# Where the lower part of a split weight is computed during the delta stage of a two-layer trunk: POOL instead of DVE

## The chip, the cores and the metric

The kernel runs on one core of a Trainium2 chip. The time is the device time of one execution in microseconds. Five engines work side by side, each through its own queue in order: PE (matrix products; its weight loads are shown apart as PEld), DVE (VectorE), ACT (ScalarE), POOL (GpSimd) and SP (which here only issues DMAs). They meet in SBUF and, for the products, in PSUM.

## The reference

Two layers over 512 latent and 256 context tokens of width 1024. Layer 0 mixes by a gated delta rule (16 value heads on 8 query/key heads of 128), layer 1 by retention; behind each stands a squared-ReLU network of width 4096. Everything is float32. What the change touches is layer 0's mixer:

```python
def gdn_mixer(hc, hl, w_in, conv_w, a_log, dt_bias, norm_g, w_out, need_ctx):
    proj = jnp.concatenate([hc, hl], axis=1) @ w_in
    qkv = proj[..., :GDN_CONV_DIM]
    z = proj[..., GDN_CONV_DIM:GDN_CONV_DIM + GDN_VALUE_DIM]
    ...
    qkv = jnp.concatenate([jax.nn.silu(short_conv(qkv[:, :n_ctx], conv_w)),
                           jax.nn.silu(short_conv(qkv[:, n_ctx:], conv_w))], axis=1)
    ...
    o = bidirectional_prefix_scan(q, k, v, g, beta, n_ctx).transpose(0, 2, 1, 3)
    ...
    y = (rmsnorm(o, norm_g) * jax.nn.silu(z)).reshape(o.shape[0], o.shape[1], GDN_VALUE_DIM) @ w_out
```

The scan works chunk by chunk. Inside a chunk it solves a unit lower triangular system, which the kernel does by inverting the triangle.

## The kernel before

**Split products.** PE multiplies in fp32r, which keeps fewer bits than float32. So every operand is split: `hi` is the value rounded to fp32r, `lo` the rest, and a product is the sum of three (hi·hi, hi·lo, lo·hi). `split` (L53) makes the two: ACT copies into `hi` (L56), DVE subtracts into `lo` (L57). For weights `w_cols` (L63) does that: it loads a block of 1024 rows and 128 columns in two halves (`raw`, 128 partitions by 512 elements, two buffers, loads on SP's queue at L72), and splits each half into a tile `hl` (three buffers). Attention to the names: `hl<-raw,hl` at L57 is the subtraction.

**The delta stage.** One call, `layer0_mix`, holds it. Its parts:

- `conv_tile` (32 times: 16 for keys and queries, 16 for values): `w_cols`, then 24 products of 512 columns into the PSUM tile `gl` and 24 of 256 into `gc`, both with two buffers (L91), then the short convolution: ACT scales one tap (L579), DVE adds three more, read straight from PSUM (L582).
- `z_tile` (16 times): the same products for the output gate, with one ACT function behind.
- `gdn_s2`, once for each pair of heads: products of keys and queries (L670), decay masks on DVE (L673, L679, L682), and the inversion of 32 by 32 triangles: their entries go through DRAM into the tile `u` (L695, L705), POOL clears the other half (L709, L711), and 30 steps of two DVE instructions each (L717, L720) follow, every one waiting for the one ahead. `gdn_iv` puts the small inverses together by products (from L754 on).
- `gdn_step`: 12 steps for each pair of heads (6 chunks in 2 directions) that carry the state. In them DVE makes `r` (L851) and `s` (L882), ACT `qs` and `und`, and POOL adds `qs` to the output of the other direction (L860).
- `gdn_y`, `gdn_y2`: norm of the output; its reciprocal root is taken on POOL (L114, tile `ms`), its product on DVE (L915), and PE transposes it (L921).

The code lists this work pair by pair with priorities (the scan first, then what the next pair needs, then projections to fill). A scheduler of the framework lays out each engine's order from the priorities and its own estimate of durations when the kernel is built, so a change of one instruction's engine changes the order on all engines. When the chip runs, each engine goes through its list strictly in order and waits wherever an operand isn't there.

Of the kernel before, what the change touches and what calls it, by code (L numbers as in the profile page):

```python
# [10 lines left out]
F32 = mybir.dt.float32  # L11
# [3 lines left out]
ALU = mybir.AluOpType  # L15
# [27 lines left out]
class Trunk:  # L43
# [6 lines left out]
            kw.setdefault("reuse_waits", "tile")  # L50
        return es.enter_context(self.tc.tile_pool(name=name, bufs=bufs, **kw))

    def split(self, hi, lo, src, scale=None):  # L53
        nc = self.nc
        if scale is None:
            nc.scalar.activation(out=hi, in_=src, func=AF.Copy)  # L56
            nc.vector.tensor_tensor(out=lo, in0=src, in1=hi.bitcast(F32), op=ALU.subtract)  # L57
        else:
            nc.scalar.activation(out=hi, in_=src, func=AF.Copy, scale=scale)
            nc.vector.scalar_tensor_tensor(  # L60
                out=lo, in0=src, scalar=scale, in1=hi.bitcast(F32), op0=ALU.mult, op1=ALU.subtract
            )

    def w_cols(self, src, parts=2):
        n = 8 // parts
        res = []
        for h in range(parts):
            raw = self.wraw.tile([128, n, 128], F32, tag="raw", name="raw")
            if callable(src):
                src(raw, h * n, n)  # L70
            else:
                self.nc.sync.dma_start(  # L72
                    out=raw, in_=src[h * n * 128:(h + 1) * n * 128].rearrange("(k p) f -> p k f", p=128))
            hl = self.whl.tile([128, 2, n, 128], F32R, tag="hl", name="hl")
            self.split(hl[:, 0], hl[:, 1], raw)
            res.append(hl)
        return lambda a, k: res[k // n][:, a, k % n, :]

# [209 lines left out]

    def layer0_mix(self):
        nc = self.nc  # L290
        es_a = ExitStack()
        es_b = ExitStack()
        self.psg = self.pool(es_a, "psg", space=PSUM)
# [5 lines left out]
        with ExitStack() as es:  # L299
# [4 lines left out]
            raw = mpool.tile([128, 8, T], F32, name="xraw")  # L304
# [35 lines left out]

        st = [{} for _ in range(8)]
        self.mark = {}
        free = ("kk0", "kk1", "uo0", "uo1")
        s1 = [self.gdn_s1(p, st[p], psk, scan, prep) for p in range(8)]
        sv = [self.gdn_sv(p, st[p], prep) for p in range(8)]
        s2 = [self.gdn_s2(p, st[p], psk, scan, prep, free if p == 0 else ("pp",) if p == 1 else ("kk0", "kk1", "uo0")) for p in range(8)]
        hi = lambda: self.tc.high_priority(PRI)
# [78 lines left out]
            fill_z()  # L426
        es_l.close()
        self.es_gdn = es_a

    def gemm_pair(self, w):  # L430
        pl = self.psg.tile([128, 512], F32, tag="gl", name="gl", bufs=2)
        self.gemm_t(pl, w, self.xt, NC_T, NL_T)
        pc = self.psg.tile([128, 256], F32, tag=self.gc[0], name="gc", bufs=self.gc[1])
        self.gemm_t(pc, w, self.xt, 0, NC_T)
        return ((pl, NC_T, NL_T), (pc, 0, NC_T))
# [942 lines left out]
```

## Time and profile before

| | |
|---|---|
| median of 3 runs | 2560.19 us (2559.29 to 2561.56) |
| profiled execution | 2564.44 us, span from the first to the last instruction 2562.7 us |
| mean granted PE clock | 0.980 |
| busy in the span: PE, DVE, ACT, POOL | 95%, 65%, 42%, 6% |
| delta stage with its projections | about 85 to 970 us of the span |

A line that names a source line, an engine and an operation stands for a group of instructions; `x` is their count, then come the busy time in us, the mean of one in ns, and behind the second bar the time that the engine idled just before them and whom it waited for. A line of windows gives a stretch (from:to and length in us) and the busy time of each engine in it with its number of instructions. Numbers such as `128x512` are partitions by elements of each.

### The profile page before, as it was taken

The numbers are of one execution on the slowest core, as the hardware profiler recorded it, in microseconds if no ns is written. First come the engines' busy times: TensorE is split into PE (matmuls) and PEld (weight loads), VectorE is DVE, ScalarE is ACT, GpSimd is POOL, SyncE is SP. The second block draws the span as 40 slices with busy tenths as digits, with TensorE's granted clock in tenths as the row PEclk, the third lists the DMA queues.
The fourth block names the chain that finished last, engine by engine and source line by source line (L and its number), as shares of the span: only waits on it lengthen the run. The fifth ranks groups of instructions, "written<-read, shape, count | busy, mean of one in ns | idle before, by whom it ended". The sixth has DMA issues, their size and how long they took to land.

```text
span 2562.7 us, 38997 instructions
## 1 busy us (share of the span) xinstructions
PE 2431.7 (95%) x14879; PEld 2010.7 (78%) x14879; DVE 1661.7 (65%) x3382; ACT 1074.0 (42%) x2357; POOL 163.7 (6%) x248
## 2 busy tenths in 40 slices
PE   8799798998888999999999999999999999999998
PEld 4687686786777787878888888888888887788887
DVE  5568767777776845887876667874353546644446
ACT  5576556565654553253222222653231322532222
POOL 1101111111201110000000000000000000000000
PEclk9899899899999999999999999999999999999999
DMA  6332324333132238354444444243122223433332
GB/s 211 89 96 77 106 51 113 80 105 94 43 109 67 74 113 272 132 165 132 132 144 129 123 130 129 100 135 93 50 84 61 78 66 115 150 97 91 107 91 91
DMA packets 346828, 276.94 MB, mean 108 GB/s; under 512 B 105608, under 2 KB 293488, under 8 KB 346640
## 3 DMA queue, kind: packets, MB, share of 16 engines
q1 hardware_dynamic: 345616, 271.30, 35.2%
q10 hardware_dynamic: 1024, 3.15, 0.5%
q8 instruction: 117, 1.92, 0.3%
q14 instruction: 71, 0.58, 0.1%
HBM read 241.72 MB, written 32.67 MB: 107 GB/s over the span
## 4 chain that ended last, share of the span: by engine, by line
PE 58%; DVE 5%; DMA 2%; ACT 2%; issue 1%; POOL 0%; SPq 0%; POOLq 0%; DVEq 0%; ACTq 0%
PE pn L940 22%; PE gl L91 14%; PE rvp L1257 5%; PE gc L91 3%; PE rl L91 3%; PE rgp L1257 3%; PE pv L1287 3%; PE sc L1265 1%; PE rc L91 1%; PE nps L276 1%; DVE hl L57 0%; DVE ma L199 0%; DMA zt<-zd 0%; PE mps L214 0%; PE uo L865 0%
## 5 line engine op out<-in xcount | busy, mean ns | idle before, releaser
L91 PE MATMUL gl<-xt,hl 128*128 128x512 f32 (+2 forms) x2760 | 704.6, 404 | 53.9 <-DVE acc L582 31.9
L91 PEld LDWEIGHTS gl<-xt,hl 128*128 128x128 f32 x2760 | 517.0, 194 | 161.9 <-issue 27.9
L57 DVE TENSOR_TENSOR hl<-raw,hl 128x1024 fp32r<-128x1024 f32 (+1 forms) x306 | 321.4, 1052 | 231.1 <-ACT hl L56 230.3
L56 ACT ACTIVATE hl<-raw 128x1024 fp32r<-128x1024 f32 (+1 forms) x306 | 280.0, 920 | 409.6 <-PE pn L940 251.9
L940 PE MATMUL pn<-hl,fh 128*128 128x512 f32 x1920 | 444.7, 391 | 2.2 <-DVE fh L1074 1.9
L940 PEld LDWEIGHTS pn<-hl,fh 128*128 128x128 f32 x1920 | 357.3, 188 | 80.0 <-DVE fh L1074 5.0
L91 PE MATMUL gc<-xt,hl 128*128 128x256 f32 x1944 | 273.2, 289 | 8.9 <-DVE acc L582 4.7
L91 PEld LDWEIGHTS gc<-xt,hl 128*128 128x128 f32 x1944 | 253.3, 193 | 19.9 <-ACT zs L442 5.5
L199 DVE SCALAR_TENSOR_TENSOR ma<-mraw,cst,ma 128x256 f32<-128x256 f32 x280 | 123.5, 482 | 40.4 <-DMA mraw<-in_w_mod 38.1
L940 PE MATMUL pn<-hl,yh 128*128 128x512 f32 x576 | 133.8, 392 | 2.5 <-ACT yh L56 1.4
L954 DVE TENSOR_TENSOR facc<-pn,facc 128x512 f32<-128x512 f32 x120 | 82.5, 689 | 81.8 <-PE pn L940 81.5
L1257 PE MATMUL rvp<-hl,xt 128*128 128x512 f32 x576 | 132.8, 389 | 0.0
L940 PEld LDWEIGHTS pn<-hl,yh 128*128 128x128 f32 x576 | 107.2, 188 | 26.8 <-ACT yh L56 2.6
L1257 PEld LDWEIGHTS rvp<-hl,xt 128*128 128x128 f32 x576 | 107.8, 188 | 22.2
L1071 ACT ACTIVATE fr<-gl 128x512 f32<-128x512 f32 x64 | 38.2, 597 | 193.3 <-PE gl L91 190.7
L582 DVE SCALAR_TENSOR_TENSOR acc<-gl,cw,acc 128x511 f32<-128x511 f32 (+1 forms) x96 | 71.6, 746 | 37.9 <-ACT acc L579 37.1
L940 PE MATMUL pn<-hl,ryt 128*128 128x512 f32 x384 | 92.0, 397 | 0.0
L1257 PE MATMUL rgp<-hl,xt 128*128 128x512 f32 x384 | 91.0, 393 | 0.0
L91 PE MATMUL rl<-xt,hl 128*128 128x512 f32 x384 | 89.5, 391 | 0.4 <-DVE hl L57 0.4
L717 DVE TENSOR_TENSOR tmp<-u 112x30 f32<-112x30 f32 (+14 forms) x240 | 81.5, 339 | 9.4 <-POOL u L709 6.2
L940 PEld LDWEIGHTS pn<-hl,ryt 128*128 128x128 f32 x384 | 71.6, 188 | 16.8
L91 PEld LDWEIGHTS rl<-xt,hl 128*128 128x128 f32 x384 | 71.5, 188 | 15.7 <-DVE hl L57 0.9
(282 smaller groups left out, 3347.9 us busy)
## 6 DMA issues: line engine op xcount, KB each, us to landing
raw<-in_w_ff SPq DMA_DIRECT2D x128, 512.0 KB
mraw<-in_w_mod SPq DMA_DIRECT2D x112, 256.0 KB
raw<-in_gdn_w_in SPq DMA_DIRECT2D x96, 256.0 KB
raw<-in_ret_w_in SPq DMA_DIRECT2D x32, 512.0 KB
mraw<-in_w_mod SPq DMA_DIRECT2D x24, 512.0 KB
e<-gd SPq DMA_DIRECT2D x32, 384.0 KB
mraw<-in_w_mod SPq DMA_DIRECT2D x8, 1024.0 KB
raw<-in_gdn_w_out SPq DMA_DIRECT2D x16, 512.0 KB
```

The source lines that it names most:

```text
L56: nc.scalar.activation(out=hi, in_=src, func=AF.Copy)
L57: nc.vector.tensor_tensor(out=lo, in0=src, in1=hi.bitcast(F32), op=ALU.subtract)
L91: nc.tensor.matmul(ps, lhsT=w(a, k), rhs=xt[:, b, k, t0:t0 + n], start=(k == 0 and i == 0), stop=(k == 7 and i == 2))
L199: eng.scalar_tensor_tensor(out=accs[v], in0=raw[:, k], scalar=c, in1=accs[v], op0=ALU.mult, op1=ALU.add)
L276: nc.tensor.transpose(ps[:, k, :], xn[:, (half * 4 + k) * 128:(half * 4 + k + 1) * 128], self.ident)
L582: nc.vector.scalar_tensor_tensor(out=acc[:, t0 + a:t0 + a + m], in0=ps[:, b:b + m], scalar=c[j], in1=acc[:, t0 + a:t0 + a + m], op0=ALU.mu ...
L717: nc.vector.tensor_tensor(out=t3, in0=u3[:, 0:c, c:c + 1].to_broadcast([112, c, n]), in1=u3[:, c:c + 1, c + 1:32].to_broadcast([112, c, n] ...
L940: m = nc.tensor.matmul(ps, lhsT=lhs(a, k, t), rhs=hls[hf][k // 2][:, b, k % 2], start=(k == 0 and n == 0), stop=(k == 3 and n == 2))
L954: nc.vector.tensor_tensor(out=dst, in0=ps, in1=dst, op=ALU.add)
L1071: nc.scalar.activation(out=r, in_=ps, func=AF.Relu)
L1257: nc.tensor.matmul(ps, lhsT=xt[:, a, kk, t * 128:(t + 1) * 128], rhs=hls[kk // 2][:, b, kk % 2], start=(kk == 0 and n == 0), stop=(kk == 7 ...
L1287: nc.tensor.matmul(pvs[it], lhsT=pts[jt][:, i, it * 128:(it + 1) * 128], rhs=v[:, j, jt], start=(jt == 0 and n == 0), stop=(jt == 5 and n ...
```

## The change

`split` takes an engine for the subtraction, and `w_cols` passes the one that stands in `self.lo_eng`. That is POOL from the first projection of the delta stage to its end, and DVE before and after it. The splits of activations and of other weights stay where they are.

```diff
-    def split(self, hi, lo, src, scale=None):
+    def split(self, hi, lo, src, scale=None, eng=None):
         nc = self.nc
         if scale is None:
             nc.scalar.activation(out=hi, in_=src, func=AF.Copy)
-            nc.vector.tensor_tensor(out=lo, in0=src, in1=hi.bitcast(F32), op=ALU.subtract)
+            (eng or nc.vector).tensor_tensor(out=lo, in0=src, in1=hi.bitcast(F32), op=ALU.subtract)
...
             hl = self.whl.tile([128, 2, n, 128], F32R, tag="hl", name="hl")
-            self.split(hl[:, 0], hl[:, 1], raw)
+            self.split(hl[:, 0], hl[:, 1], raw, eng=self.lo_eng)
...
     def layer0_mix(self):
         nc = self.nc
+        self.lo_eng = None
...
         self.mark = {}
+        self.lo_eng = nc.gpsimd
...
         self.es_gdn = es_a
+        self.lo_eng = None
```

In the changed file the delta stage's lines have numbers that are higher by two in `layer0_mix` and by three behind it: L709 is L712 there, L720 is L723.

This is POOL's order before, where the inversion of the fifth pair of heads begins; `off` are off-diagonal blocks copied for `gdn_iv`, `e` the masked products they come from, and the digits are buffer numbers:

```order
L699 COPY off_4351<-e_4023 64x768
L702 COPY off_4350<-e_4023 32x384 x2
L699 COPY off_4351<-e_4038 64x768
L702 COPY off_4350<-e_4038 32x384 x2
L709 AFFINE_SELECT u<-u 112x1024
L711 MEMSET u 112x32
L114 TENSOR_TENSOR ms<-ms,mhalf 128x4
L860 TENSOR_TENSOR o<-o,qs 128x256 x2
L114 TENSOR_TENSOR ms<-ms,mhalf 128x4
```

And the same place of POOL's order in the changed kernel:

```order
L57 TENSOR_TENSOR hl<-raw,hl 128x512 x2
L702 COPY off_4351<-e_4023 64x768
L705 COPY off_4350<-e_4023 32x384 x2
L702 COPY off_4351<-e_4038 64x768
L705 COPY off_4350<-e_4038 32x384 x2
L57 TENSOR_TENSOR hl<-raw,hl 128x512 x3
L712 AFFINE_SELECT u<-u 112x1024
L714 MEMSET u 112x32
L57 TENSOR_TENSOR hl<-raw,hl 128x512 x3
L114 TENSOR_TENSOR ms<-ms,mhalf 128x4
L863 TENSOR_TENSOR o<-o,qs 128x256 x2
L57 TENSOR_TENSOR hl<-raw,hl 128x512 x2
```

Three subtractions stand ahead of the select that opens the inversion, three behind it, and two behind the scan's additions.

DVE's order at the same place, before: the last transposes ahead of the inversion, results `mrow` of another small job, and the inversion's first three instructions:

```order
L691 STREAM_TRANSPOSE btt<-e_4038 32x384 x4
L236 TENSOR_TENSOR mrow<-mps_3977,mrow 2x128
L57 TENSOR_TENSOR hl<-raw,hl 128x512
L236 TENSOR_TENSOR mrow<-mps_3977,mrow 2x128
L57 TENSOR_TENSOR hl<-raw,hl 128x512
L582 SCALAR_TENSOR_TENSOR acc<-gl,cw,acc 128x510
L57 TENSOR_TENSOR hl<-raw,hl 128x512
L717 TENSOR_TENSOR tmp<-u 112x30
L582 SCALAR_TENSOR_TENSOR acc<-gl,cw,acc 128x511
L720 TENSOR_TENSOR u<-u,tmp 112x30
L582 SCALAR_TENSOR_TENSOR acc<-gl,cw,acc 128x511
L717 TENSOR_TENSOR tmp<-u 112x58
```

And in the changed kernel:

```order
L694 STREAM_TRANSPOSE btt<-e_4038 32x384 x4
L236 TENSOR_TENSOR mrow<-mps_3977,mrow 2x128
L585 SCALAR_TENSOR_TENSOR acc<-gl,cw,acc 128x510
L585 SCALAR_TENSOR_TENSOR acc<-gl,cw,acc 128x511 x2
L720 TENSOR_TENSOR tmp<-u 112x30
L723 TENSOR_TENSOR u<-u,tmp 112x30
L720 TENSOR_TENSOR tmp<-u 112x58
```

The three subtractions are gone, and the convolution's three additions, which were interleaved with the inversion's first steps, stand ahead of it.

## The prediction

> **What bounds the kernel now.** The view by windows comes first, cut at the stage borders: projection and delta stage (85 to 970 us; the first weight tiles and the set-up lie before it), output projection, feed-forward, retention, second feed-forward.
>
> ```profile
> 85.00:970.00 885.00, 791.33 (x7068) 661.09 (x7069) 634.59 (x1614) 512.78 (x1414) 127.74 (x184) 0.95 0.32 88
> 970.00:1147.00 177.00, 171.42 (x802) 141.15 (x801) 130.05 (x201) 66.82 (x122) 4.31 (x6) 0.98 0.57 186
> 1147.00:1640.00 493.00, 489.57 (x2511) 418.36 (x2510) 357.69 (x699) 150.04 (x256) 1.50 (x4) 1.00 0.42 129
> 1640.00:2200.00 560.00, 554.45 (x2567) 455.58 (x2566) 309.07 (x534) 186.12 (x333) 15.82 (x29) 1.00 0.28 85
> 2200.00:2562.00 362.00, 353.76 (x1589) 291.54 (x1587) 179.60 (x223) 112.22 (x157) 2.74 (x5) 1.00 0.34 106
> ```
>
> The columns are the length, then PE, weight load, DVE, ACT and POOL busy, the granted clock and the DMA. Behind 970 us PE is busy 97 to 99% at full clock, and the change touches nothing there. In the delta stage PE is idle for 885 - 791 = 94 us, DVE is busy 72%, POOL 14%, and the clock is 0.95: if the low state is half speed, 10% of the stage, 88 us, ran at half, which costs up to 44 us. So the most that any change to this stage could bring is about 94 + 44 us, and PE stays the bound. Who keeps PE waiting there is in the view of waits, cut to the stage (us in total, times, longest):
>
> ```profile
> PE gl L91 <- DVE acc L582: 31.9, 11, 9.1
> PE yps L921 <- DVE o L915: 6.7, 8, 1.5
> PE ivps L754 <- DVE v L745: 6.3, 3, 5.9
> PE gl L91 <- DVE hl L57: 5.4, 3, 3.1
> PE gl L91 <- ACT hl L56: 5.1, 3, 4.2
> PE gc L91 <- DVE acc L582: 4.7, 2, 4.2
> PE mps L232 <- DVE mrow L236: 3.9, 1, 3.9
> PE uo L865 <- DVE r L851: 2.6, 4, 1.2
> ```
>
> The seven DVE rows add to 61.5 us, two thirds of PE's idle time. Most of it is not the subtraction that moves (5.4 us) but the convolution's readers of the projection's PSUM banks: they stand late in DVE's queue, and PE cannot reuse the bank. The gain, if there is one, is that DVE reaches these sooner.
>
> **What leaves DVE.**
>
> ```profile
> L57 DVE TENSOR_TENSOR hl<-raw,hl 128x512 fp32r<-128x512 f32 x98 | 67.4, 690 | 32.7 <-ACT hl L56 32.4
> L679 DVE TENSOR_TENSOR qkd<-qm,e 128x512 f32<-128x512 f32 x48 | 35.3, 735 | 15.8 <-ACT e L657 15.2
> L682 DVE TENSOR_TENSOR e<-kkps,e 128x512 f32<-128x512 f32 x48 | 32.9, 686 | 0.7
> L717 DVE TENSOR_TENSOR tmp<-u 112x30 f32<-112x30 f32 (+14 forms) x240 | 81.5, 339 | 9.4 <-POOL u L709 6.2
> L720 DVE TENSOR_TENSOR u<-u,tmp 112x30 f32<-112x30 f32 (+14 forms) x240 | 81.1, 338 | 3.6
> L915 DVE TENSOR_TENSOR o<-o,ms 128x512 f32<-128x512 f32 x24 | 17.6, 733 | 14.0 <-POOL ms L114 13.9
> ```
>
> Of the 98 subtractions of this size 96 are moved (32 convolution tiles and 16 gate tiles, two halves each; the other two belong to the decay columns, ahead of the stage): 96 x 0.690 = 66.2 us off DVE.
>
> **What POOL pays.** The trace has no 128x512 subtraction on POOL; it has two-input ones of 256 and of 12 elements a partition.
>
> ```profile
> L860 POOL TENSOR_TENSOR o<-o,qs x48: 721/728/1665, 201.3 to 938.9; 128x256 f32<-128x256 f32 x48
> L619 POOL TENSOR_TENSOR we<-egl,rk 128x12 f32<-128x12 f32 x16 | 3.6, 242 | 0.6
> ```
>
> From 242 ns at 12 to 728 ns (the median) at 256 is 1.99 ns an element, so 512 take 728 + 256 x 1.99 = 1.24 us; doubling 728 gives 1.46 us as the upper end. That the output is fp32r should cost nothing: on DVE the row writing it (690) is as long as the equal one that writes f32 (686). I take 1.24 us: 96 x 1.24 = 119 us more on POOL, 247 of 885 us busy, so POOL is no bound. The Trainium skill, GPSIMD Engine Reference, section 4.1 Engine selection, speaks against the move: two-input elementwise work belongs on VectorE, being about twice as slow on GPSIMD. The same page, section 3 Performance versus the Vector engine, gives 4497 ns for 2048 elements, of which a quarter is 1.12 us (an estimate); by that the sum below would gain about 3 us of DVE time.
>
> **What DVE pays for it: the port.** Two engines at one moment, in the timeline:
>
> ```profile
> 741.43 0.27 DVE L720 TENSOR_TENSOR u<-u,tmp 112x108 f32<-112x108 f32 x1
> 741.74 0.78 DVE L717 TENSOR_TENSOR tmp<-u 112x84 f32<-112x84 f32 x1
> 741.68 0.73 POOL L860 TENSOR_TENSOR o<-o,qs 128x256 f32<-128x256 f32 x1 [0.74 <-ACT qs L856]
> ```
>
> POOL's addition began 0.06 us before the DVE product of 84 columns, which then took 0.78 us where the longer one ahead of it took 0.27: it stood still until POOL was done. It reads two operands from SBUF. L682, with one operand in PSUM, has a mean of 686 ns, against 735 for L679 of the same shape with both in SBUF. So I take it that a POOL subtraction holds off only the DVE instructions with two SBUF inputs: L717, L720, L679 and L915, 552 of them once the 96 are gone.
>
> They are not spread evenly. The eight triangular inversions (60 alternating L717 and L720 each) fill eight stretches. These are the first, the last and the sum of all engines in them, and below them the first, the last and the sum of the moved subtractions on DVE in the same stretches:
>
> ```profile
> 132.20:166.20 34.00, 32.28 (x188) 28.34 (x187) 28.92 (x84) 22.48 (x45) 2.59 (x6) 1.00 0.30 87
> 829.60:866.20 36.60, 33.89 (x206) 26.59 (x205) 32.21 (x107) 21.12 (x71) 3.79 (x6) 1.00 0.29 85
> sum 287.40, PE 262.94 PEld 220.17 DVE 253.78 ACT 189.11 POOL 29.55; mean PE 32.87 PEld 27.52 DVE 31.72 ACT 23.64 POOL 3.69
> ...
> 132.20:166.20 34.00, 4.13 (x6) 1.00 0.30 87
> 829.60:866.20 36.60, 1.38 (x2) 1.00 0.29 85
> sum 287.40, DVE 20.77; mean DVE 2.60
> ```
>
> *Inside the stretches* DVE is busy 253.8 of 287.4 us and 480 two-input instructions start, 1.67 a microsecond. If POOL's 1.24 us fall at random, the part of them in which DVE has not yet met such an instruction is (1 - e^(-1.67 x 1.24)) / 1.67 = 0.52 us; it stands for the other 0.72 us. Now 20.8 / 0.69 = 30 subtractions lie there. Each costs DVE 0.72 in place of 0.69: nothing is won, 30 x 0.03 = 1 us is lost. Bounds: no blocking wins 21 us, full blocking loses 30 x 0.55 = 17 us. I stay with 0.72, since the row at 741.74 shows a hit that waits nearly the whole addition.
>
> *Outside* there are 66 of the 96, and L679 and L915, 72 instructions in 598 us, 0.12 a microsecond: 0.12 x 1.24² / 2 = 0.09 us each. DVE wins 66 x (0.69 - 0.09) = 39 us there. Its load goes from 634.6 - 253.8 = 381 to 342 of 598 us.
>
> **From DVE's load to the time.** No row gives this step. The waits come from bursts in a queue, and a queue's lag goes about with busy over idle time: outside 381/217 = 1.76 before, 342/256 = 1.34 after, 24% less. PE's idle time is 24.5 us inside the stretches and 70 outside, so three quarters of the 61.5 us, 46 us, shrink by 24%: **-11 us**. Inside: **+1**. The clock's 44 us shrink with the idle time that causes them: two thirds of it waits for DVE, three quarters of that outside, 24% of this: **-5**. Against this, each half of a weight tile is ready 1.24 - 0.69 = 0.55 us later. In the waits above six rows' events hang on it (three L57, three L56): 6 x 0.55 = 3.3, and about as much again for a subtraction that waits its turn behind other POOL work, in all **+5**, bounded by 0 (there is room in the three buffers) and 96 x 0.55 = 53. The sum is -10 us.
>
> The Trainium skill, TensorE: Matmul & The Clock Gate, Part 1, says the clock falls to half only after about 3.4 us without work; by that a 9.1 us gap that shrinks by a quarter wins no clock, the -5 would be nearly 0, and the sum -5. The window's 0.95 cannot tell the two apart.
>
> Two POOL instructions lie on DVE's path, and the new order puts subtractions ahead of them.
>
> ```profile
> L709 POOL TENSOR_SCALAR_AFFINE_SELECT u<-u 112x1024 f32<-112x1024 f32 x8 | 10.5, 1312 | 50.9 <-DMA u<-ud 50.9
> SPq L72 <- DVE hl L57: 175.5, 31, 22.5
> ```
>
> The select that starts each inversion follows three subtractions in the fifth head pair, 3.7 us, but POOL idled 50.9 / 8 = 6.4 us there for the DMA: covered, and if the cover goes, up to 8 x 3.7 = 30 us of inversions start late. The weight loads on SP's queue waited 175.5 us for DVE to free a raw buffer; they will wait for POOL, later by the 0.55 us counted above. The loads themselves and the bytes are the same.
>
> The profiled execution took 2564.4 us (its span is 2562.7 and 1.7 lies around it): 2564.4 - 10 = 2554. The median of the runs is 4.2 us lower, so I forecast **2550 us**.
>
> **Rivals.** *Nothing measurable* (chance 0.25; a measurement of this kernel tells apart about 0.2%, 5 us): PE's larger waits are single bursts, and each holds few of the subtractions, so the lighter mean load does not shorten them; the gain of 16 and the cost of 6 fall to about 4 each: 2560. For it speaks that only 5.4 us of PE's waits name the subtraction. Against it, that two thirds of the idle time names DVE.
>
> *Slower through the port* (0.20): more of the subtractions fall into the inversions than do now. The new POOL order has three right behind the start of most of them, and more between the next additions. With five an inversion, 40 in all, each blocking for its whole 1.24 us, the stretches grow by 40 x 1.24 - 21 = 29 us; DVE's 34 us of idle time there are waits for PE and ACT and don't absorb it. This decides from the point where PE runs out of filling projections while the inverse is late (now 6.3 us at L754). Less 16 outside and plus 5: +18, 2578. The Trainium skill, SBUF — State Buffer, section Who interferes with whom, says that the second to issue blocks fully until the first is done, which is this price.
>
> *Slower through POOL's order* (0.08): a subtraction queued behind an addition L860 that waits for the scan. If one in eight, 12, comes 3 us late for PE, +36 less 16: 2580.
>
> That the move doesn't happen is excluded: the new POOL order holds 96 subtractions, and DVE's holds 96 fewer.
>
> **How the numbers follow.** The forecast has 0.47, its own range is 2535 to 2555. Faster by over 0.2% takes that 0.47, within it 0.25, slower the two last, 0.28. The range 2530 to 2578 reaches from the case without any blocking (21 us off the stretches, taken at half) to the price of the port, and leaves out about 2 in 10.
>
> **What would show it.** L57 on POOL at 1.2 to 1.3 us where DVE leaves it alone, 1.5 and more inside the inversions. L717, L720, L679 longer in the mean, by some 22 + 6 us together. DVE busy about 600 us in the stage. PE's waits for L582 down from 37 to about 28 us, its waits for L57 at most a few us more. Stages behind the delta stage equal in length. The forecast is wrong if PE's waits for hl or for L754 grow past 15 us, if the inversions' stretches get longer by over 2 us each, or if POOL's subtraction takes over 1.5 us when nothing blocks it.

## The result and the profile after

| | before | after |
|---|---|---|
| median | 2559.74 us, 4 runs (2558.84 to 2561.56) | 2573.07 us, 4 runs (2572.47 to 2575.93) |
| profiled execution | 2564.44 us, span 2562.7 us | 2573.55 us, span 2571.8 us |
| mean granted PE clock | 0.980 | 0.982 |

The ratio is 1.0051 with a 95% interval of 1.0036 to 1.0066: slower by 0.5%, 13 us, and clear of the noise, where 2550 us had been forecast.

The view by windows of the kernel after, at the same five borders. The delta stage's end is moved by 8 us, since its projections are done that much later (columns as before: length, then PE, weight load, DVE, ACT and POOL busy, clock, DMA).

```profile
85.00:978.00 893.00, 789.84 (x7066) 655.66 (x7065) 620.86 (x1522) 506.89 (x1408) 242.73 (x275) 0.96 0.32 88
978.00:1155.00 177.00, 170.68 (x796) 140.20 (x796) 127.80 (x199) 66.41 (x121) 4.39 (x6) 0.98 0.57 185
1155.00:1648.00 493.00, 490.12 (x2514) 418.71 (x2513) 357.71 (x699) 149.96 (x257) 1.51 (x4) 1.00 0.42 129
1648.00:2208.00 560.00, 553.93 (x2564) 454.98 (x2562) 308.08 (x531) 185.74 (x331) 15.86 (x29) 1.00 0.28 85
2208.00:2571.00 363.00, 354.34 (x1590) 292.07 (x1590) 180.68 (x226) 112.81 (x158) 2.76 (x5) 0.99 0.34 106
```

The four later stages have their old lengths within 1 us. The delta stage is 8 us longer, and PE, with the same products, is idle there for 893 - 790 = 103 us in place of 94. (The profiled runs differ by 9 us and the medians by 13, since the profiled run of before lies 5 us above its median.) DVE's busy time fell from 634.6 to 620.9 us, not to 600. Where the difference went is in the groups of the whole page:

```profile
L57 POOL TENSOR_TENSOR hl<-raw,hl 128x512 fp32r<-128x512 f32 x96 | 129.0, 1349 | 330.9 <-ACT hl L56 279.3 <-DVE xt L177 18.3 <-DMA tt<-vd 13.5
L723 DVE TENSOR_TENSOR u<-u,tmp 112x30 f32<-112x30 f32 (+14 forms) x240 | 99.7, 415 | 4.7
L720 DVE TENSOR_TENSOR tmp<-u 112x30 f32<-112x30 f32 (+14 forms) x240 | 90.2, 376 | 22.2 <-POOL u L712 18.1
L682 DVE TENSOR_TENSOR qkd<-qm,e 128x512 f32<-128x512 f32 x48 | 37.8, 787 | 18.2 <-ACT e L660 17.6
L685 DVE TENSOR_TENSOR e<-kkps,e 128x512 f32<-128x512 f32 x48 | 32.9, 686 | 0.9
L918 DVE TENSOR_TENSOR o<-o,ms 128x512 f32<-128x512 f32 x24 | 21.8, 906 | 12.8 <-POOL ms L114 12.8
L712 POOL TENSOR_SCALAR_AFFINE_SELECT u<-u 112x1024 f32<-112x1024 f32 x8 | 10.1, 1269 | 4.4 <-DMA u<-ud 4.4
```

The kernel has three lines more, so L720 is the old L717, L723 the old L720, L682 the old L679, L585 the old L582. The four groups with two SBUF inputs became longer by 8.7 + 18.6 + 2.5 + 4.2 = 34 us; L685, with one operand in PSUM, stayed at 686 ns to the nanosecond. Two idle times changed: DVE waits 18.1 us for POOL's select (6.2 before), and the select itself hardly waits for its DMA any more (4.4 against 50.9): POOL is now often still at other work when the DMA has landed. The view of waits of PE in the stage:

```profile
PE gc L91 <- DVE acc L585: 17.0, 5, 7.6
PE gl L91 <- DVE acc L585: 16.4, 7, 4.7
PE gl L91 <- ACT hl L56: 9.4, 2, 9.0
PE yps L924 <- DVE o L918: 9.2, 8, 2.0
PE knps L819 <- DVE mrow L236: 8.6, 2, 5.0
PE gl L91 <- DVE tmp L720: 7.4, 2, 5.5
PE kk L878 <- ACT und L873: 7.4, 6, 5.3
PE gl L91 <- POOL hl L57: 6.6, 9, 1.2
```

The wait for `acc` that was to shrink from 36.6 to 28 us is still 33.4 us, and there are waits for the inversion's `tmp` and for POOL's `hl` that did not exist. SP's queue, lastly, waits 305.3 us for POOL to free `raw`, where it waited 175.5 us for DVE.

The eight stretches of the inversions, from the first `tmp` to the last `u` of each, have this sum:

```profile
sum 290.90, PE 228.62 PEld 187.02 DVE 261.38 ACT 172.15 POOL 68.28; mean PE 28.58 PEld 23.38 DVE 32.67 ACT 21.52 POOL 8.53
```

They are only 3.5 us longer than before (287.4), and 34 of POOL's subtractions lie in them. But PE, busy for 262.9 us of them before, is now idle in them for 62 us in place of 24, and in the rest of the stage for 41 us in place of 69.

Nothing in this tells the cause: the scheduler laid out all engines anew, so most waits stand at other places, and three explanations fit.

- **Order:** the new order is dearer, and the move of the subtraction alone is not.
- **Port:** POOL's reading of two inputs holds up DVE in the inversions.
- **Late weights:** the lower part comes later, or POOL, occupied, does its other work later.

### The profile page after: what moved, and what is told of

It reads as the page before. It is cut to its first block, busy times and chain, and to the rows that moved or that the text cites. A ratio compares the mean times of both kernels' runs of the same rounds, so it can differ in the third digit from the quotient of the medians.

```text
span 2571.8 us, 39004 instructions
## 1 busy us (share of the span) xinstructions
PE 2430.2 (94%) x14879; PEld 2005.2 (78%) x14879; DVE 1644.3 (64%) x3286; ACT 1068.5 (42%) x2353; POOL 288.0 (11%) x344
## 3 DMA queue, kind: packets, MB, share of 16 engines
q10 hardware_dynamic: 1024, 3.15, 0.5%
## 4 chain that ended last, share of the span: by engine, by line
PE 64%; DVE 9%; issue 3%; DMA 3%; ACT 2%; POOL 1%; SPq 0%; POOLq 0%; DVEq 0%; ACTq 0%
PE pn L943 23%; PE gl L91 15%; PE rvp L1260 5%; PE gc L91 4%; PE rl L91 3%; PE rgp L1260 3%; PE pv L1290 2%; PE sc L1268 1%; PE uo L868 1%; DVE u L723 1%; PE rc L91 1%; PE kk L878 1%; DVE tmp L720 1%; PE uo L889 1%; DMA mraw<-in_w_mod 1%
## 5 line engine op out<-in xcount | busy, mean ns | idle before, releaser
L91 PE MATMUL gl<-xt,hl 128*128 128x512 f32 (+2 forms) x2760 | 696.2, 401 | 48.1 <-DVE acc L585 16.4
L57 DVE TENSOR_TENSOR hl<-raw,hl 128x1024 fp32r<-128x1024 f32 (+1 forms) x210 | 255.3, 1217 | 200.2 <-ACT hl L56 199.4
L57 POOL TENSOR_TENSOR hl<-raw,hl 128x512 fp32r<-128x512 f32 x96 | 129.0, 1349 | 330.9 <-ACT hl L56 279.3
L585 DVE SCALAR_TENSOR_TENSOR acc<-gl,cw,acc 128x511 f32<-128x511 f32 (+1 forms) x96 | 71.5, 745 | 51.6 <-ACT acc L582 44.5
L720 DVE TENSOR_TENSOR tmp<-u 112x30 f32<-112x30 f32 (+14 forms) x240 | 90.2, 376 | 22.2 <-POOL u L712 18.1
L723 DVE TENSOR_TENSOR u<-u,tmp 112x30 f32<-112x30 f32 (+14 forms) x240 | 99.7, 415 | 4.7
```

What stands on the lines that cost most here:

```text
L57: (eng or nc.vector).tensor_tensor(out=lo, in0=src, in1=hi.bitcast(F32), op=ALU.subtract)
L91: nc.tensor.matmul(ps, lhsT=w(a, k), rhs=xt[:, b, k, t0:t0 + n], start=(k == 0 and i == 0), stop=(k == 7 and i == 2))
L585: nc.vector.scalar_tensor_tensor(out=acc[:, t0 + a:t0 + a + m], in0=ps[:, b:b + m], scalar=c[j], in1=acc[:, t0 + a:t0 + a + m], op0=ALU.mu ...
L720: nc.vector.tensor_tensor(out=t3, in0=u3[:, 0:c, c:c + 1].to_broadcast([112, c, n]), in1=u3[:, c:c + 1, c + 1:32].to_broadcast([112, c, n] ...
L723: nc.vector.tensor_tensor(out=u3[:, 0:c, c + 1:32], in0=u3[:, 0:c, c + 1:32], in1=t3, op=ALU.subtract)
```

## The experiments

Most experiments fix the order, so that only one thing differs. Every instruction of an engine is chained to the next one in a given list; such a chain is an order within an engine and adds no wait between engines. "Old order" below means PE, DVE, ACT, SP and POOL's other work exactly as in the kernel before. The kernel before was timed again beside each group of runs (medians 2560.4 to 2562.2 us), and the ratios are to that.

| run | subtraction, order | median us | ratio to before (95%) |
|---|---|---|---|
| e1 | POOL, old order | 2583.12 | 1.0081 (1.0068 to 1.0093) |
| e2 | DVE, order of after | 2600.86 | 1.0161 (1.0144 to 1.0178) |
| e3 | short fill on POOL, old order | 2547.02 | 0.9948 (0.9934 to 0.9961) |
| e4 | long fill on POOL, old order | 2571.31 | 1.0037 (1.0023 to 1.0051) |
| e5 | 63 on POOL, outside the inversions, old order | 2563.23 | 1.0008 (0.9999 to 1.0017) |
| e6 | 33 on POOL, inside them, old order | 2585.20 | 1.0090 (1.0074 to 1.0107) |
| e7 | as e5, order left to the scheduler | 2573.14 | 1.0046 (1.0034 to 1.0059) |
| e8 | fill as long as the subtraction, old order | 2559.98 | 0.9994 (0.9985 to 1.0002) |
| e9 | as e1, the select ahead of a subtraction | 2578.91 | 1.0071 (1.0059 to 1.0083) |
| e10 | as e5, the select ahead | 2565.73 | 1.0023 (1.0013 to 1.0033) |
| e11 | on DVE and once more on POOL, old order | 2604.58 | 1.0175 (1.0162 to 1.0188) |
| e12 | short fill, then POOL busy elsewhere, old order | 2556.76 | 0.9982 (0.9970 to 0.9994) |

### Engine and order apart: e1, e2

e1 is the changed kernel with the old order; e2 is the kernel before with the order of after. (The list of the order and the function that chains it are not shown here.)

```diff
         trunk_kernel(tc, *aps, out)
+        _force(tc, nc)
```

> The 96 subtractions on POOL as in the changed kernel, but every other instruction of PE, DVE, ACT, SP and POOL in exactly the order of the kernel before; only the place of the 96 on POOL is new. Three theories. Order: the scheduler's new order costs the 13 us, and the move alone does not; then this run is at or below 2560 us (2545 to 2560), and PE's waits for acc fall below the 36.6 us of the kernel before. Port: POOL's subtraction holds up DVE's two-input instructions (34 us in the changed kernel) and the inversions with them; then 2566 to 2580, with the eight inversion stretches longer than 287 us by 5 to 15 us. Late weights: the lower halves come later, and buffers with them; then 2566 to 2580, with PE waits for hl of 10 us or more.

> The other corner: the 96 subtractions stay on DVE as in the kernel before, but every other instruction of the five engines has exactly the order of the changed kernel. Order: 2573 us or more (2573 to 2590), since DVE carries 66 us more in the order that is the dearer one. Port and late weights: what costs is gone, so 2555 to 2563 us, about the kernel before.

e1 took 2583 us, 21 us more than before, and more than the changed kernel itself. So in the old order the move alone costs, and "order" as the cause falls; 2583 us is 3 above the range of the other two. e2 took 2601 us, above every range set for it: the order of after is a bad one for a kernel that subtracts on DVE (39 us), though it is the better one by 8 (ratios) to 10 us (medians) for a kernel that subtracts on POOL. An order and an engine belong together; neither has a price by itself: in the order of after, the same move from DVE to POOL wins 28 us (2601 to 2573). The experiments that follow take the move apart in the old order, in which the prediction had reckoned; none of them was done in the order of after.

The inversion stretches of e1 (the sum of all engines in them):

```profile
sum 306.20, PE 266.94 PEld 220.77 DVE 268.71 ACT 186.56 POOL 73.94; mean PE 33.37 PEld 27.60 DVE 33.59 ACT 23.32 POOL 9.24
```

They are 306.2 us long, 18.8 more than before's 287.4: nearly all of the 21 us. DVE, which has some 30 subtractions less to do in them, is busy for 15 us more. PE's waits for POOL's `hl` are 1.3 us in this run, not the 10 that late weights called for.

### What in POOL's work costs: e3, e4, e8, e12

e3 replaces the subtraction by a fill of the lower part, behind the same ACT copy.

```diff
-            nc.scalar.activation(out=hi, in_=src, func=AF.Copy)
-            (eng or nc.vector).tensor_tensor(out=lo, in0=src, in1=hi.bitcast(F32), op=ALU.subtract)
+            up = nc.scalar.activation(out=hi, in_=src, func=AF.Copy)
+            if eng is None:
+                nc.vector.tensor_tensor(out=lo, in0=src, in1=hi.bitcast(F32), op=ALU.subtract)
+            else:
+                m = eng.memset(lo.bitcast(F32).unsqueeze(1).to_broadcast([128, 1] + list(lo.shape[1:])), 0.0)
+                self.tc.add_manual_dep(m.ins, up.ins.name, ...)
```

> As the run with POOL in the old order, instruction for instruction on all five engines, but each of the 96 POOL subtractions is a POOL fill of the lower part with a constant, which reads nothing from SBUF and is shorter (the lower part of these weights is left out of the result). Port: DVE's held-up time goes, so this run is 8 us or more below the run with POOL in the old order. Late weights: a few us below it, and the waits of SP for POOL's hl shorter. Order: within 3 us of it.

2547 us, 36 us below e1 and 13 to 15 below the kernel before. So there is something to win by taking the work off DVE; what POOL does in its place gives it back and more. The fill is also shorter (525 ns), and it gives `raw` back earlier, so the run doesn't yet tell port from lateness. e4 makes the fill longer than the subtraction:

```diff
-                m = eng.memset(lo.bitcast(F32).unsqueeze(1).to_broadcast([128, 1] + list(lo.shape[1:])), 0.0)
+                m = eng.memset(lo.bitcast(mybir.dt.uint8), 0)
```

> As the run with the short POOL fill (525 ns each, 2547 us), same order on all engines, but the fill writes the lower part byte by byte, 2048 elements in place of 512, so that it should last about 2.1 us (4 x 525 ns), longer than the subtraction's 1.3 us, and still reads nothing from SBUF (the lower part of these weights is left out of the result). Port: what POOL reads at the same time as DVE is what costs, not how long the lower part takes; then 2545 to 2556 us and inversion stretches of 280 to 290 us in sum. Late weights: the lower part is ready 0.8 us later than with the subtraction, so this run is at or above the 2583 us of POOL's subtraction in the old order.

It lasted 1.81 us, less than reckoned, and the run took 2571 us: neither theory's number, but halfway. DVE was not held up at all (the two groups of the inversion 79.8 and 81.0 us, before 81.5 and 81.1), and yet a POOL that is longer busy costs. Both causes are there, so e8 makes the fill as long as the subtraction and gives `raw` back at the same point (the copy puts one column of the raw weights into the lower part, only so that `raw` is held until then):

```diff
+                m = eng.memset(lo[:, 0:2].bitcast(F32), 0.0)
+                self.tc.add_manual_dep(m.ins, up.ins.name, ...)
+                eng.memset(lo[:, 2:4].bitcast(mybir.dt.uint8), 0)
+                eng.tensor_copy(out=lo[:, 3, 127:128], in_=src[:, 3, 127:128])
```

> Old order on all engines. In place of each POOL subtraction stands a POOL fill of about the same length (a word fill of one half of the tile, a byte fill of the other, then a copy of one column of raw, so that raw is given back when it was): by the two fills measured, 0.26 + 0.90 us and some 0.15 for the copy, 1.3 us in all (the lower part of these weights is left out of the result). POOL is as long busy and the lower part as late as with the subtraction's 1.32 us; only the reading of two inputs is gone. If the 36 us between the short fill (2547) and the subtraction (2583) are lateness alone: 2578 to 2585. If they are the held-up DVE alone: 2545 to 2552. Both, as the long fill lets one expect (24 us for 1.28 us more): 2547 + 0.8 x 19 = 2562, range 2555 to 2570, with DVE's instructions as short as before.

2560 us, as expected from "both", although the three parts (medians 0.31 + 0.95 + 0.18 = 1.44 us) are even a little longer than the subtraction (median 1.29, mean 1.32). Between e8 and e1 only the reading differs, apart from this slightly longer work of POOL in e8, and e1 is 1.0081 - 0.9994 = 0.9% slower, 22 us. The same beginning of the sixth inversion in both kernels shows how; first e1, from the timeline (start, duration, instruction):

```profile
627.27 0.21 DVE L720 TENSOR_TENSOR tmp<-u 112x30 f32<-112x30 f32 x1 [9.28 <-POOL u L712]
627.30 0.16 POOL L714 MEMSET u<- 112x32 f32 x1
627.42 1.29 POOL L57 TENSOR_TENSOR hl<-raw,hl 128x512 fp32r<-128x512 f32 x1
627.51 1.27 DVE L723 TENSOR_TENSOR u<-u,tmp 112x30 f32<-112x30 f32 x1
...
629.60 0.24 DVE L723 TENSOR_TENSOR u<-u,tmp 112x84 f32<-112x84 f32 x1
629.62 1.37 POOL L57 TENSOR_TENSOR hl<-raw,hl 128x512 fp32r<-128x512 f32 x1 [0.91 <-ACT hl L56]
...
629.88 1.25 DVE L720 TENSOR_TENSOR tmp<-u 112x108 f32<-112x108 f32 x1
```

and then e8:

```profile
607.38 0.21 DVE L728 TENSOR_TENSOR tmp<-u 112x30 f32<-112x30 f32 x1 [10.21 <-POOL u L720]
...
607.48 0.31 POOL L60 MEMSET hl<- 128x256 f32 x1
607.62 0.22 DVE L731 TENSOR_TENSOR u<-u,tmp 112x30 f32<-112x30 f32 x1
607.73 0.95 POOL L64 MEMSET hl<- 128x1024 uint8 x1
607.88 0.22 DVE L728 TENSOR_TENSOR tmp<-u 112x58 f32<-112x58 f32 x1
608.13 0.22 DVE L731 TENSOR_TENSOR u<-u,tmp 112x58 f32<-112x58 f32 x1
```

In e1 the second instruction of the chain, 0.22 us of work, takes 1.27 us: it ends when POOL's subtraction does. The seventh does so again. In e8 the same instructions run at their own speed beside a POOL that is just as busy. The two groups of the inversion over the whole run, first in e1, then in e8:

```profile
L720 DVE TENSOR_TENSOR tmp<-u 112x30 f32<-112x30 f32 (+14 forms) x240 | 92.5, 386 | 26.4 <-POOL u L712 22.9
L723 DVE TENSOR_TENSOR u<-u,tmp 112x30 f32<-112x30 f32 (+14 forms) x240 | 97.1, 405 | 4.3
...
L728 DVE TENSOR_TENSOR tmp<-u 112x30 f32<-112x30 f32 (+14 forms) x240 | 81.1, 338 | 28.4 <-POOL u L720 22.4 <-DMA zd<-zs 2.5
L731 DVE TENSOR_TENSOR u<-u,tmp 112x30 f32<-112x30 f32 (+14 forms) x240 | 80.8, 337 | 4.3
```

The sum over the eight stretches of e8:

```profile
sum 283.20, PE 257.42 PEld 215.64 DVE 238.75 ACT 186.43 POOL 77.66; mean PE 32.18 PEld 26.95 DVE 29.84 ACT 23.30 POOL 9.71
```

From e8 to e1 the stretches grow by 23.0 us, DVE's busy time in them by 30.0, and the kernel by 22. So in the old order practically the whole price of the port is paid in the inversions.

e12 takes up the rest, the 13 us between the short and the equal fill. Lower part early, POOL busy as long:

```diff
+                m = eng.memset(lo.bitcast(F32), 0.0)
+                self.tc.add_manual_dep(m.ins, up.ins.name, ...)
+                eng.memset(src[:, 0:2].bitcast(mybir.dt.uint8), 0)
```

> Old order on all engines. Each POOL subtraction is replaced by a short word fill of the lower part (0.53 us, then PE may read it) and behind it a byte fill of half of the raw tile, which nobody reads any more (0.95 us): 1.48 us of POOL in all, as with the equal fill, raw given back as late, nothing read from SBUF (the lower part of these weights is left out of the result). If the 13 us between the short fill (2547) and the equal fill (2560) are the lateness of the lower part: 2545 to 2551. If they come from POOL being occupied, so that its other work starts later, or from raw given back later: 2556 to 2563.

2556.8 us: a lower part that is ready 0.95 us earlier is worth about 3 us (0.9994 - 0.9982; the intervals overlap, so it may be nothing), and the larger share, some 9 us (0.9982 - 0.9948), comes from POOL being occupied or from `raw` given back later. These two were not told apart by a run of their own. But e4 and e3 say something on it: in both, SP's waits for `raw` name ACT's copy (184 and 176 us), not POOL, so `raw` is given back alike, and still e4 with 1.28 us more per fill is 23 us slower (1.0037 - 0.9948). A late `raw` is thus not needed for a busy POOL to cost.

### Where it costs: e5, e6, e7

Of the 96 subtractions 33 ran on DVE inside or at the rim of the inversion stretches of the kernel before. e5 gives the 63 others to POOL, e6 these 33 (e5's edit is shown; in e6 `in` stands for `not in`).

```diff
+            eng = None
+            if self.lo_eng is not None:
+                eng = self.lo_eng if self.lo_n not in IN_INVERSION else None
+                self.lo_n += 1
-            self.split(hl[:, 0], hl[:, 1], raw, eng=self.lo_eng)
+            self.split(hl[:, 0], hl[:, 1], raw, eng=eng)
```

> Old order on all engines; POOL takes the 63 subtractions that ran outside the eight inversion stretches in the kernel before, the 33 inside stay on DVE at their old places. Port: the stretches are as long as before (282 to 292 us in sum, against 306 with all 96 on POOL) and the 63 x 0.69 us off DVE help a little: 2545 to 2560 us. Late weights: two thirds of the 21 us of all 96 remain: 2570 to 2580.

> The complement: old order, POOL takes only the 33 subtractions that ran inside the inversion stretches, the 63 others stay on DVE. Port: the stretches grow by the same 19 us as with all 96 and nothing is won outside: 2578 to 2592 us. Late weights: a third of the 21 us: 2565 to 2572.

The 33 cost 23 us, all that the 96 cost (stretches 304.2 us). The 63 cost nothing that can be measured (stretches 290.3 us), which refutes late weights as the main cause; but they win nothing either, and e5 misses the range of the port theory by 3 us. That POOL's longer occupation gives back what DVE is spared outside would fit e12, but was not tested here.

> The same 63 outside subtractions on POOL and 33 on DVE, but with the order left to the scheduler, as in the changed kernel. Port: with the dear ones back on DVE it is below the changed kernel's 2573; if the new order is also the better one for POOL's part, below 2562: 2545 to 2565. Late weights or an order that is dear by itself: 2570 or more.

2573 us, as the changed kernel, and 10 us more than the old order with the same engines (e5): by its expectation the port theory missed. The trace shows, though, that the 63 did not stay outside. Left to the scheduler, 15 of them ran on POOL inside the inversion stretches (4 in e5), the two groups of the inversion took 172.3 us (165.3 in e5), and the stretches measure 298.8 us in sum (290.3 in e5). So the run does not test what it was meant to; that these 8.5 us are the cause of the 10 is not shown. It does say that the order must be laid out, or kept, with care in any version of this.

### The cover of the select, and a candidate: e9, e10

In six of eight places POOL's select, which starts an inversion, stood right behind a subtraction. e9 changes POOL's list of e1 there, e10 that of e5 in five places (`hl_2171`: the number of the buffer):

```diff
-L57 TENSOR_TENSOR hl_2171<-raw_2169,hl_2171 128x512
 L712 AFFINE_SELECT u_606<-u_606 112x1024
 L714 MEMSET u_606 112x32
+L57 TENSOR_TENSOR hl_2171<-raw_2169,hl_2171 128x512
```

> All 96 subtractions on POOL in the old order, but POOL's select on u, which starts each inversion, stands ahead of the one subtraction that it stood behind in six of eight places. If the lost cover counts (DVE waited 22.9 us for the select against 6.2 before): 2565 to 2578 us, with that wait below 10 us. If it stood beside other waits: within 4 us of 2583.

> The 63 outside subtractions on POOL, 33 on DVE, old order, and the select ahead of one subtraction in five places: a candidate to beat both kernels. DVE's wait for the select falls from 11.1 us to below 8; 2550 to 2560 us if this cover was what ate the gain, 2563 if not.

In e9 DVE's wait for the select fell from 22.9 to 14.7 us, less than expected, and the time by 0.1%, with intervals that overlap. So the lost cover is real on DVE, but what e9 gave back of it is worth 3 us by the ratios, which is within the noise. In the candidate e10 the wait fell from 11.1 to 8.6 us, and the time is no better than e5's. No version that leaves nothing out was faster than the kernel before.

### The port without the relief: e11

DVE keeps its subtraction, and POOL does it once more into `raw`, which nobody reads any more.

```diff
             nc.vector.tensor_tensor(out=lo, in0=src, in1=hi.bitcast(F32), op=ALU.subtract)
+            if eng is not None:
+                eng.tensor_tensor(out=src, in0=src, in1=hi.bitcast(F32), op=ALU.subtract)
```

> The kernel before in its own order, all 96 subtractions on DVE, and POOL does each of them once more behind DVE, in place on the raw tile, which nobody reads after it. Nothing is taken off DVE and no lower part comes later; what is added is POOL's reading of two inputs (and raw is given back some 1.3 us later). Port: DVE's held-up instructions grow by 25 to 45 us in sum and the time by 15 to 30 us: 2577 to 2592. Lateness alone: 2560 to 2566.

2605 us: 1.75% slower, beyond the range. The held-up groups grew by 25.6 us, at the lower end of what was expected, the subtractions still on DVE, which read two inputs as well, by another 5 (741 ns each in place of 690), and the stretches from 287 to 312 us, so 25 of the 45 us lie where the port theory puts them. The rest lies outside. There `raw` comes back after both subtractions, SP waits 319 us for POOL to free it, and ACT waits 24.8 us for the raw weights (6.9 before). That this makes up all of the rest was not tested.

## Why the prediction was wrong, step by step

By ratios of about 2561 us, the old order first:

| term of the sum | predicted | measured |
|---|---|---|
| inside the inversions: work taken off DVE | -21 | -5 (stretches of e3: 282.4 for 287.4) |
| inside: DVE held up | +22 | +22 (e8 to e1) |
| outside: lighter DVE, with the clock | -16 | -8 (rest of e3's -13) |
| lower part later | +5 | +3 (e12 to e8) |
| POOL's other work and `raw` later | 0, covered | +9 (e3 to e12) |
| new order | not in the sum | -8 (e1 to after) |
| **sum** | **-10** | **+13** |

The measured terms add up by construction: each is the step from one run to the next on the way from before over e3, e12, e8 and e1 to after. Each is uncertain by some 4 to 5 us, and another way would divide the 13 us otherwise: over e2 they are +41 for the order and -28 for the engine.

- **What bounds the kernel, and the four later stages:** right. **96 subtractions, 66 us off DVE:** right. **POOL's 1.24 us:** right, the median is 1.28. (Inside the stretches of the changed kernel it is 1.34 us in the mean, 45.5 us for 34, not the 1.5 and more that was expected there.)
- **The port as a mechanism:** right, with its size. 34 us of DVE held up in the changed kernel and 31 in e1, against 28. The Trainium skill, SBUF — State Buffer, section Who interferes with whom, says that a DVE instruction with two SBUF inputs contends with a GpSimd instruction that reads SBUF and not with one that only writes. The runs agree on both halves: the inversion's two groups take 189.6 us beside e1's subtractions, 161.9 beside e8's fills of the same length, which read one column, and 160.8 beside e4's, which read nothing.
- **The step that failed** is "inside the stretches": each subtraction "costs DVE 0.72 in place of 0.69: nothing is won, 30 x 0.03 = 1 us is lost". It set DVE's time against DVE's time, as if both counted alike for the length of a stretch. They do not. From before to e8 DVE has 15.0 us less to do in the stretches, its idle time there grows from 33.6 to 44.5 us, and the stretches shrink by 4.2. From e8 to e1 it has 30.0 us more, its idle time falls by 7.0, and they grow by 23.0. What took up the difference stands in DVE's waits, added over the eight stretches: the scan's `s`, which lies in DVE's queue between links of the inversion, waited 5.5 us for PE's `kk` before, 13.7 in e8 and 6.6 in e1. So time taken off DVE here mostly became a longer wait for PE, and a quarter of it came through; of the time added to the links, that wait took back 7 us, and three quarters came through. In the old order the term was +17, not +1.
- **From DVE's load to the time outside:** right in direction, half the size: -8 for -16. The clock's share of -5 is not shown: the runs of e3 had mean granted clocks of 0.980 to 0.985, those of the kernel before beside them 0.981 to 0.982. In the changed kernel the wait for `acc` fell to 33.4 us, not 28.
- **The cover of the select:** wrong. The select waited 6.4 us for its DMA on average, but in five of eight places of e1 POOL was still at a subtraction, which had waited for ACT, when the DMA had landed. The price is small, by e9. The larger cost, of a busy POOL or a late `raw` (9 us), was not in the sum.
- **The rival "slower through the port"** had the mechanism and nearly the time (2578 against 2573, and 2583 in the old order). In the old order it had the place too; in the changed kernel, whose stretches grew by 3.5 us and not by its 29, the near hit of the number is in part luck. Its condition, that 40 subtractions must fall into the inversions, wasn't needed: the 33 that lay there do it.
- **The order** was not in the sum. The scheduler's new one won back 8 of the 21 us. Whether the port costs as much in that order is open: there, 34 us of DVE were held up, but no run took the reading alone out of it.

## What to carry to other kernels

Ask of each piece of work that is moved what the engine will wait for in its place; if another wait takes up the time, little is won when it goes. On POOL a two-input instruction was paid twice here, once there and once by the two-input DVE instructions beside it (31 us of them in e1), so keep it away from serial chains on DVE. Test such a move with the order held still, and with a stand-in of the same length that does not read the two inputs: the first tells the engine from the order, the second the port from the rest. And when the order is left free, look in the trace where the moved pieces went.

## What the runs showed of the hardware

POOL's fills take their time by the element, not by the byte: 128 x 512 words 525 ns, 128 x 2048 bytes (the same memory) 1805 ns, 128 x 1024 bytes 951 ns. These are the lines of e3, e4 and e8, cut to the stage, which holds 91 of the 96:

```profile
L60 POOL MEMSET hl<- 128x512 f32 x91 | 47.8, 525 | 318.7 <-ACT hl L56 294.4 <-PE kk L884 13.9 <-issue 9.1
L60 POOL MEMSET hl<- 128x2048 uint8 x91 | 163.1, 1805 | 267.9 <-ACT hl L56 232.5 <-issue 25.1 <-PE gc L97 4.6
L64 POOL MEMSET hl<- 128x1024 uint8 x91 | 86.6, 951 | 0.0
```

Even 1.8 us long they left DVE's two-input instructions at their own speed (160.8 us for the inversion's two groups in e4, 162.6 before).
